# A first stage in five uneven groups of k-tiles, and a small inverse whose last transfers go through GpSimd's queue

## The chip, the cores and the metric

The kernel runs on one core of a Trainium2 chip. The metric is the device time of one execution in microseconds (us), as the median of several runs. Beside the timed runs there is one profiled execution with a trace, and a page that sums it up; all durations of single instructions come from it.

The engines are TensorE (PE, with PEld for its weight loads), VectorE (DVE), ScalarE (ACT), GpSimd (POOL) and SyncE (SP). Each works through its own queue in order. A transfer (DMA) is issued by an engine's queue: here nearly all by SP, a few by ACT. An instruction that waits holds all that stands behind it on its queue.

## What is computed

One layer of a streaming encoder on 512 prompt tokens and 64 sample tokens, of width 2048, all in float32. Cut to what matters:

```
mod = silu(c) @ w_ada + b_ada             # shift and scale (sh1, sc1), four more vectors
h = rmsnorm(x, norm1) * (1 + sc1) + sh1
proj = h @ w_in                           # columns: aq, ak, av, ar, alr, bq, bk, bv, bg, ...
o_a = GLA(aq, ak, av, gates)              # 4 heads, 64-frame blocks
o_b = GDN(bq, bk, bv, gates)              # 8 heads, each with a triangular solve (I + L)^-1
x = x + g1 * (concat(o_a, o_b) @ w_out)
x = x + g2 * conv_ffn(rmsnorm(x, norm2) * (1 + sc2) + sh2)
y = rmsnorm(x, final_norm)
```

A float32 product is made of three products of parts: each operand is split into a high part in fp32r and a low rest, and high x high, high x low and low x high are summed in PSUM.

## The kernel before, in words

Weights and activations are tiled in k-tiles of 128 rows; D = 2048 gives 16 of them. The 576 tokens are two halves of 288 columns. The function mm6 multiplies one weight tile (128x128, split in wh and wl) with one k-tile of h (split in hh and hl): six matmuls of 288 columns.

**The first stage** is the function head. It does three things at once:

- x: five blocks of tokens (four of 128, one of 64) are loaded, squared on ACT for the mean square (x_square, L765), scaled on DVE (x_scale, L769 to L772, with a power on POOL between) and turned by PE (x_turn, L780), with copies out of PSUM by ACT (L783) and DVE (L785, L788). The result is xT, x transposed.
- Modulation: the first 4096 columns of w_ada (shift and scale for norm1) are loaded in tiles called hraw, 512 KB each, from a pool of N_HRAW buffers. The generator modulation(g) does, for one group of columns, eight steps: each multiplies four k-tiles (L830), then the sums are copied out, turned, reduced, and the biases are added (L838 to L846).
- Early products: six heads of the projection (EARLY: one of bq, three of aq, two of ak) are multiplied here, in pairs of heads. They need h, made by make(k) (split_mod, L664 to L668) out of xT and of the modulation of k's own group.

Because the modulation of a group of k-tiles is enough for the products over these k-tiles, the stage goes by groups: four groups of four k-tiles. While group g is multiplied, modulation(g + 1) is stepped between the products (next(mods)). Weights of a pair are loaded by pair_load (L934) and split by pair_split (L942, L943); w_ahead(n) says how many pairs are asked for. The sums over groups are added by sum_early (L952, L957), and at the last group the results are stored (L959, L960). A narrow product (narrow_w, mm_narrow, L1050) gives the gates. load_vectors loads seven groups of small vectors by rows (v_load, L702) and turns them into columns by PE (v_turn, L710, L711).

**The mixers** follow, from about 184 to 1150 us. Weight tiles go through wtile (load L737 by SP, split on ACT and DVE, multiplied by mm6), and after each mm6 a planner is called (tick). It keeps an estimated clock, steps the jobs (generators of the heads' work) when their estimated times are due, and so writes one fixed order of instructions for every engine. Its estimate of a transfer is DMA_US + n x ISSUE_US per wait, in the function moved. The rest of w_ada's columns is summed beside it on DVE (ada_blocks; loads L976 by SP).

Each GDN head inverts a triangular 128x128 matrix. Its 16x16 diagonal blocks are inverted on POOL in inverse16: the matrix is stored to DRAM (L411), its blocks are loaded so that 32 blocks lie in 32 partitions (L418), fourteen pairs of steps run on POOL (L425, L426, shown at the helper's line L1961), a copy makes the transposed inverse (L428), then both are stored to DRAM (d1, L430) and loaded in another order into the tile cm (L435), which DVE spreads into the tiles u and t (L441, shown at L1931). PE goes on with them (shown at L1947). There are nine such inverses: eight heads and one for the samples. All of these transfers are issued by SP's queue:

```
nc.sync.dma_start(d1.rearrange("w q f -> q w f"), lane)
...
for w in range(2):
    nc.sync.dma_start(cm[:, w], d1[w].rearrange("(b n) (i j) -> (n i) b j", b=4, i=16))
```

POOL also makes the powers of every norm (rsqrt, L151) and masks; the wrapper _InTurn (L1961) keeps all of these in program order.

tc.issue_after(ins) puts what is traced inside it behind ins on the queue of the engine of ins. It is an order of issue on that one engine; it adds no wait for another.

## Time and profile before

| what | value |
|---|---|
| median of 3 runs | 2891.37 us (2891.16 to 2893.65) |
| profiled execution | 2892.92 us, span 2890.8 us |
| mean granted TensorE clock | 0.987 |
| busy share PE, PEld | 97%, 95% |
| busy share DVE, ACT, POOL | 71%, 41%, 11% |
| instructions | 52029 |
| moved by transfers | 395.53 MB, 137 GB/s on average |

The span goes from the first to the last instruction; the execution's own time is 2.1 us longer. Busy shares are averages over stages with different limits. In rows of stretches stand the stretch, its length, then for PE, PEld, DVE, ACT and POOL the busy time and the number of instructions, then the granted TensorE clock (1.00 is full), the busy share of the 16 DMA engines and GB/s. Rows of the timeline have start, duration, engine, line, operation, output <- inputs, count, and in brackets the idle time before and what ended it. In rows that group instructions stand the shapes, the count, then busy us and mean ns of one, then idle time. Rows of one tile show minimum, median and maximum in ns. Names such as "m" or "bank" are those of tiles, their numbers left out.

### The profile page before, as it was taken

The numbers are of one execution on the slowest core, as the hardware profiler recorded it, in microseconds if no ns is written. First come the engines' busy times: TensorE is split into PE (matmuls) and PEld (weight loads), VectorE is DVE, ScalarE is ACT, GpSimd is POOL, SyncE is SP. The second block draws the span as 40 slices with busy tenths as digits, with TensorE's granted clock in tenths as the row PEclk, the third lists the DMA queues.
The fourth block names the chain that finished last, engine by engine and source line by source line (L and its number), as shares of the span: only waits on it lengthen the run. The fifth ranks groups of instructions, "written<-read, shape, count | busy, mean of one in ns | idle before, by whom it ended". The sixth has DMA issues, their size and how long they took to land.

```text
span 2890.8 us, 52029 instructions
## 1 busy us (share of the span) xinstructions
PE 2811.7 (97%) x20964; PEld 2733.9 (95%) x20964; DVE 2059.6 (71%) x3305; ACT 1185.4 (41%) x2031; POOL 330.1 (11%) x513
## 2 busy tenths in 40 slices
PE   6999999999999999999999999999999999999998
PEld 3799999999899989999999999999999999999997
DVE  3468787688787783478888888888888855555555
ACT  4246544453544442454444444444444422212123
POOL 0003252323020000000111111111111000000000
PEclk8999999999999999999999999999999999999999
DMA  8966446545655555433333333333333553333221
GB/s 293 309 180 182 140 141 184 142 131 168 187 144 147 165 152 149 145 98 108 106 102 113 107 108 100 108 108 112 108 100 108 192 176 100 111 104 113 84 79 66
DMA packets 535444, 395.53 MB, mean 137 GB/s; under 512 B 59657, under 2 KB 465412, under 8 KB 535204
## 3 DMA queue, kind: packets, MB, share of 16 engines
q1 hardware_dynamic: 527860, 390.54, 44.9%
q8 instruction: 165, 2.70, 0.4%
q10 hardware_dynamic: 7344, 1.67, 0.3%
q14 instruction: 75, 0.61, 0.1%
HBM read 356.47 MB, written 35.67 MB: 136 GB/s over the span
## 4 chain that ended last, share of the span: by engine, by line
PE 87%; DVE 3%; DMA 3%; POOL 3%; issue 2%; ACT 1%; SPq 0%; ACTq 0%; POOLq 0%; DVEq 0%
PE g L641 29%; PE g L643 14%; PE bank L1584 12%; PE bank L1583 11%; PE bank L1585 11%; PE bank L1947 5%; POOL m L1961 3%; PE bank L1943 1%; DVE acc L1931 1%; PE bank L830 1%; DVE wl L1931 1%; DMA m<-gd 0%; ACT m L1907 0%; DMA raw<-in_w_in_dram 0%; PE ps_nar L1050 0%
## 5 line engine op out<-in xcount | busy, mean ns | idle before, releaser
L1584 PE MATMUL bank<-slot,wh 128*128 128x290 f32 x2464 | 739.0, 300 | 0.0
L1583 PE MATMUL bank<-slot,wh 128*128 128x290 f32 x2464 | 735.1, 298 | 0.0
L1585 PE MATMUL bank<-slot,wl 128*128 128x290 f32 x2464 | 728.8, 296 | 0.0
L641 PE MATMUL g<-slot,wh 128*128 128x288 f32 x3168 | 551.6, 295 | 0.3 <-DVE slot L1931 0.3
L641 PE MATMUL g<-hh,wh 128*128 128x288 f32 x2048 | 474.7, 313 | 5.4 <-ACT wh L1931 4.4
L1585 PEld LDWEIGHTS bank<-slot,wl 128*128 128x128 f32 x2464 | 471.8, 191 | 0.0
L1584 PEld LDWEIGHTS bank<-slot,wh 128*128 128x128 f32 x2464 | 468.8, 190 | 0.1
L641 PEld LDWEIGHTS g<-slot,wh 128*128 128x128 f32 x3168 | 464.2, 188 | 0.7 <-DVE slot L1931 0.5
L1583 PEld LDWEIGHTS bank<-slot,wh 128*128 128x128 f32 x2464 | 463.9, 188 | 0.1
L1931 ACT ACTIVATE wh<-raw 128x1024 fp32r<-128x1024 f32 x215 | 227.6, 1059 | 545.5 <-PE g L641 537.6
L641 PE MATMUL g<-hl,wh 128*128 128x288 f32 x2048 | 443.4, 298 | 0.0
L643 PE MATMUL g<-hh,wl 128*128 128x288 f32 x2048 | 443.2, 298 | 0.0
L1931 DVE SCALAR_TENSOR_TENSOR slot<-g,mod,slot 128x512 f32<-128x512 f32 (+1 forms) x448 | 201.7, 491 | 304.2 <-PE g L643 303.0
L641 PEld LDWEIGHTS g<-hh,wh 128*128 128x128 f32 x2048 | 328.4, 191 | 28.4 <-issue 14.2
L643 PE MATMUL g<-slot,wl 128*128 128x288 f32 x1584 | 342.1, 295 | 0.0
L641 PEld LDWEIGHTS g<-hl,wh 128*128 128x128 f32 x2048 | 332.9, 190 | 3.4 <-issue 2.5
L643 PEld LDWEIGHTS g<-hh,wl 128*128 128x128 f32 x2048 | 330.9, 190 | 2.4 <-issue 2.4
L1931 DVE TENSOR_TENSOR wl<-raw,wh 128x1024 fp32r<-128x1024 f32 x215 | 262.5, 1221 | 28.1 <-ACT wh L1931 25.1
L1530 ACT ACTIVATE wh<-raw 128x1024 fp32r<-128x1024 f32 x176 | 186.1, 1057 | 225.7 <-PE bank L1584 190.1
L643 PEld LDWEIGHTS g<-slot,wl 128*128 128x128 f32 x1584 | 255.5, 188 | 0.0
L1531 DVE TENSOR_TENSOR wl<-raw,wh 128x1024 fp32r<-128x1024 f32 x176 | 215.3, 1223 | 54.1 <-ACT wh L1530 54.1
L1530 ACT ACTIVATE wh<-s 128x1024 fp32r<-128x1024 f32 x132 | 140.2, 1062 | 210.5 <-DVE s L1541 109.2
(319 smaller groups left out, 3316.9 us busy)
## 6 DMA issues: line engine op xcount, KB each, us to landing
raw<-in_w_up_dram SPq DMA_DIRECT2D x176, 512.0 KB
raw<-in_w_in_dram SPq DMA_DIRECT2D x100, 512.0 KB
raw<-in_w_down_dram SPq DMA_DIRECT2D x88, 512.0 KB
aw<-in_w_ada_dram SPq DMA_DIRECT2D x71, 512.0 KB
hraw<-in_w_ada_dram SPq DMA_DIRECT2D x64, 512.0 KB
xr<-in_w_ada_dram SPq DMA_DIRECT2D x57, 512.0 KB
raw<-in_w_out_dram SPq DMA_DIRECT2D x32, 512.0 KB
slot<-actd SPq DMA_DIRECT2D x44, 288.0 KB
```

The lines of the kernel that those rows point to most:

```text
L641: T.matmul(ps[:, h if bank is None else bank, :n], wh, x[:, h, :n], start=f, stop=False)
L643: T.matmul(ps[:, h if bank is None else bank, :n], wl, ah[:, h, :n], start=False, stop=stop)
L830: T.matmul(ps[32 * k:32 * k + 32], cs[:, k0 + k], got[n][k // 2][:, k % 2], start=(k0 == 0), stop=(k0 == KD - 4))
L1530: self.nc.scalar.activation(hi, src, AF.Copy)
L1531: self.nc.vector.tensor_tensor(lo, src, hi.bitcast(F32), op=ALU.subtract)
L1583: T.matmul(ps, wh[:, j], hi, start=(c < 3 and j == 0), stop=False, skip_group_check=True)
L1584: T.matmul(ps, wh[:, j], lo, start=False, stop=False, skip_group_check=True)
L1585: T.matmul(ps, wl[:, j], hi, start=False, stop=(j == NPAIR - 1), skip_group_check=True)
L1931: return f(*a, **kw)
L1943: return self.engine.transpose(out, *a)
L1947: return self.engine.matmul(out, *a, **kw)
L1961: r = f(*a, **kw)
```

## The change

The first stage: GROUPS makes five groups of 2, 3, 4, 4 and 3 k-tiles. Group 0 then needs 256 columns each of scale and shift; its w_ada tiles hold four k-tiles of 256 columns, the others two k-tiles of the group's width. There are nine hraw buffers for eight, and ada_fill asks for w_ada as far as eight of them reach, with the weights of the next group's pairs put between (w_ahead). The first pair of weights and the narrow weights are asked for before x is squared. x_scale is cut in two (x_norm: mean and power; x_scale: four multiplications on DVE); x_square runs two blocks ahead; issue_after fixes that x's transposes come behind the last modulation step, that ACT's copies come behind a given number of squares, and that the next block's scaling on DVE comes in the middle of a block's turn. Modulation steps are spread evenly over the products (ten calls over a group). Vector group 1 is loaded later, groups 2 to 6 during the first two groups of products, into other places.

The inverse: the store of d1 and the loads of cm are issued by GpSimd's queue, the loads in four pieces instead of two. What the planner is told (moved) stays as it was.

The diff, cut to its core (what is left out does the same with the group's width and place in transposes, sums, pair_split and narrow_w, which becomes narrow_load and narrow_split):

```diff
@@ -38,13 +38,14 @@
...
-N_HRAW, HRAW_AHEAD = 8, 3
+N_HRAW = 9
...
+GROUPS = ((0, 2), (2, 3), (5, 4), (9, 4), (13, 3))
@@ -427,12 +428,14 @@
...
-        nc.sync.dma_start(d1.rearrange("w q f -> q w f"), lane)
+        nc.gpsimd.dma_start(d1.rearrange("w q f -> q w f"), lane)
...
-            nc.sync.dma_start(cm[:, w], d1[w].rearrange("(b n) (i j) -> (n i) b j", b=4, i=16))
+            for h in range(2):
+                nc.gpsimd.dma_start(cm[:, w, 2 * h:2 * h + 2],
+                                    d1[w, 16 * h:16 * h + 16].rearrange("(b n) (i j) -> (n i) b j", b=2, i=16))
@@ -763,40 +767,48 @@
...
-        def x_scale(b):
+                squared.append(last())
...
+        def x_norm(b):
...
+        def x_scale(b):
+            n, m = P if b < 4 else TS, ms[b]
...
-        def x_turn(b):
+        def x_turn(b, middle):
...
-                    T.transpose(ps[:, (k - k0) * n:(k - k0 + 1) * n], xt[b][k // 4][:n, k % 4 * P:(k % 4 + 1) * P],
-                                self.c["ident"][:n, :n])
+                    with self.tc.issue_after(summed[0]) if summed else nullcontext():
+                        T.transpose(ps[:, (k - k0) * n:(k - k0 + 1) * n], xt[b][k // 4][:n, k % 4 * P:(k % 4 + 1) * P],
+                                    self.c["ident"][:n, :n])
...
-                if b < 4:
-                    put(xT[:, k0:k0 + per, b // 2, (b % 2) * P:(b % 2 + 1) * P], ps.rearrange("p (k t) -> p k t", k=per))
-                else:
-                    for h in range(2):
-                        put(xT[:, k0:k0 + per, h, HP:HT], ps.rearrange("p (k h t) -> p k h t", k=per, h=2)[:, :, h])
+                ahead = 4 * b + (8 if k0 // per < 2 else 10)
+                with self.tc.issue_after(squared[min(len(squared), ahead) - 1]):
+                    if b < 4:
+                        put(xT[:, k0:k0 + per, b // 2, (b % 2) * P:(b % 2 + 1) * P], ps.rearrange("p (k t) -> p k t", k=per))
+                    else:
+                        for h in range(2):
+                            put(xT[:, k0:k0 + per, h, HP:HT], ps.rearrange("p (k h t) -> p k h t", k=per, h=2)[:, :, h])
+                if k0 // per == 1 and middle is not None:
+                    with self.tc.issue_after(last()):
+                        middle()
...
+        self.load_consts(self.cp, LONG)
...
-        self.load_consts(self.cp, LONG)
...
-        v_load(1)
...
-        v_turn(1)
@@ -807,19 +819,33 @@
...
-        todo = [(g, mi, k0) for g in range(4) for mi in (1, 0) for k0 in range(0, KD, 4)]
+        todo = [(g, mi, k0) for g in range(len(GROUPS)) for mi in (1, 0) for k0 in range(0, KD, 4)]
...
+        per_tile = lambda g: 4 if GROUPS[g][1] == 2 else 2
...
-                c0 = mi * D + g * 512
-                got[j] = [hraw().rearrange("p (k n) -> p k n", k=2) for _ in range(2)]
+                (m0, nm), per = GROUPS[g], per_tile(g)
+                c0, w = mi * D + m0 * P, nm * P
+                got[j] = [hraw()[:, :per * w].rearrange("p (k n) -> p k n", k=per) for _ in range(4 // per)]
...
-                    k1 = k0 + 2 * h
-                    nc.sync.dma_start(raw, i["w_ada"][0, k1 * P:(k1 + 2) * P, c0:c0 + 512].rearrange("(k p) n -> p k n", p=P))
+                    k1 = k0 + per * h
+                    nc.sync.dma_start(raw, i["w_ada"][0, k1 * P:(k1 + per) * P, c0:c0 + w].rearrange("(k p) n -> p k n", p=P))
...
+        def ada_fill():
+            while len(got) < len(todo):
+                if len(got) % 8 == 0:
+                    g = len(got) // 8
+                    w_ahead(3 if g == 1 else 3 * g - 2)
+                held = sum(len(x) for x in got.values() if x)
+                if held + 4 // per_tile(todo[len(got)][0]) > N_HRAW - 1:
+                    return
+                ada_ahead(len(got) + 1)
...
+            (m0, nm), per = GROUPS[g], per_tile(g)
+            w = nm * P
@@ -827,51 +853,60 @@
...
-                        T.matmul(ps[32 * k:32 * k + 32], cs[:, k0 + k], got[n][k // 2][:, k % 2], start=(k0 == 0), stop=(k0 == KD - 4))
+                        T.matmul(ps[32 * k:32 * k + 32, :w], cs[:, k0 + k], got[n][k // per][:, k % per], start=(k0 == 0), stop=(k0 == KD - 4))
...
+                summed[:] = [last]
...
-                ada_ahead(n + 1 + HRAW_AHEAD)
+                ada_fill()
...
-        first = modulation(0)
-        ada_ahead(1)
-        x_load(3)
-        ada_ahead(2)
-        x_load(4)
-        for g in (2, 3, 4):
-            v_load(g)
-        late = [lambda: v_turn(2), lambda: v_turn(3), lambda: v_load(5), lambda: v_turn(4), lambda: v_load(6), lambda: v_turn(5), lambda: v_turn(6)]
-        for b in range(5):
-            if b == 0:
-                x_square(0)
-            x_scale(b)
-            if b < 4:
-                x_square(b + 1)
-            x_turn(b)
-            if b > 0:
-                next(first)
-        for _ in first:
-            pass
...
-        pairs = [(g, e) for g in range(4) for e in range(0, len(EARLY), 2)]
...
+        pairs = [(g, e) for g in range(len(GROUPS)) for e in range(0, len(EARLY), 2)]
...
-                raws[j] = self.pair_load([off + h * P for _, off, h in EARLY[e:e + 2]], 4 * g)
+                raws[j] = self.pair_load([off + h * P for _, off, h in EARLY[e:e + 2]], *GROUPS[g]), GROUPS[g][1]
...
+        first, summed = modulation(0), []
+        ada_ahead(2)
+        x_load(3)
+        x_load(4)
+        ada_ahead(4)
+        v_load(1)
+        ada_ahead(7)
+        w_ahead(1)
+        nar = self.narrow_load(*GROUPS[0])
+        x_square(0)
+        x_norm(0)
+        x_scale(0)
+        x_square(1)
+        for b in range(5):
+            if b < 4:
+                x_norm(b + 1)
+            if b < 3:
+                x_square(b + 2)
+            x_turn(b, (lambda b=b: x_scale(b + 1)) if b < 4 else None)
+            if b > 0:
+                next(first)
+            if b == 3:
+                v_turn(1)
+        for _ in first:
+            pass
+        nar = self.narrow_split(pool, nar)
+        late = [lambda g=g: v_turn(g) for g in range(2, 7)]
@@ -883,26 +918,34 @@
...
-        nar = self.narrow_w(pool, 0)
-        for g in range(4):
-            mods = modulation(g + 1) if g < 3 else iter(())
-            ks = range(4 * g, 4 * g + 4)
+        for g, (m0, nm) in enumerate(GROUPS):
+            ks = range(m0, m0 + nm)
+            end = g == len(GROUPS) - 1
+            mods = iter(()) if end else modulation(g + 1)
+            units = nm * len(EARLY)
+            done = stepped = 0
...
+            def product(e, j, k):
+                nonlocal done, stepped
+                self.mm6(ps[j], w[j][0][:, k - m0], w[j][1][:, k - m0], self.h[k], k == m0, k == ks[-1])
+                done += 1
+                while stepped < 10 and stepped * (units - nm) < 10 * done:
+                    next(mods, None)
+                    stepped += 1
...
-                w = self.pair_split(raws[3 * g + e // 2])
+                w = self.pair_split(*raws[3 * g + e // 2])
...
-                        self.mm_narrow(k, nar[:, k % 4])
+                        self.mm_narrow(k, nar[:, k - m0])
...
-                            self.mm6(ps[j], w[j][0][:, k % 4], w[j][1][:, k % 4], self.h[k], k == 4 * g, k == 4 * g + 3)
+                            product(e, j, k)
...
-                        next(mods, None)
-                        if late:
-                            late.pop(0)()
-                    if g == 3:
+                    if end:
@@ -910,38 +953,39 @@
...
-                    if e == 4 and g < 3 and j == 0:
-                        nar = self.narrow_w(pool, 4 * g + 4)
+                    if e == 4 and not end and j == 0:
+                        nar = self.narrow_split(pool, self.narrow_load(*GROUPS[g + 1]))
...
-                        if e == 4 and g < 3 and j == 1 and k % 2 == 0:
-                            make(4 * g + 4 + k % 4 // 2)
-                        self.mm6(ps[j], w[j][0][:, k % 4], w[j][1][:, k % 4], self.h[k], k == 4 * g, k == 4 * g + 3)
-                        if k % 2 == 1:
-                            next(mods, None)
-                        if k == ks[1]:
-                            if late:
-                                late.pop(0)()
-                            if j == 0:
-                                w_ahead(3 * g + e // 2 + 3)
+                        if e == 4 and not end and j == 1 and k - m0 < 2:
+                            make(len(self.h))
+                        product(e, j, k)
+                        if g == 0 and e == 4:
+                            v_load(2 + 2 * j + k)
+                        if g == 1 and e == 2 and late:
+                            late.pop(0)()
+                        if k == ks[1] and j == 0:
+                            w_ahead(3 * g + e // 2 + 3)
...
+            if g == 0:
+                v_load(6)
...
-    def pair_load(self, offs, k0):
...
-        raw = self.raw()
+    def pair_load(self, offs, k0, n):
...
+        raw, w = self.raw(), n * P
...
-            self.nc.sync.dma_start(raw[:, e * 512:(e + 1) * 512].rearrange("p (k n) -> p k n", k=4), self.w_in(off)(k0, k0 + 4))
+            self.nc.sync.dma_start(raw[:, e * w:(e + 1) * w].rearrange("p (k n) -> p k n", k=n), self.w_in(off)(k0, k0 + n))
...
-    def pair_split(self, raw):
...
-        nc = self.nc
-        hi, lo = [self.wq.tile([P, 1024], F32R, tag="w" + c, bufs=3, name=self.name("w" + c)) for c in "hl"]
+    def pair_split(self, raw, n):
...
+        nc, w = self.nc, n * P
+        hi, lo = [self.wq.tile([P, 1024], F32R, tag="w" + c, bufs=3, name=self.name("w" + c))[:, :2 * w] for c in "hl"]
...
-            nc.scalar.activation(hi, raw, AF.Copy)
-            nc.vector.tensor_tensor(lo, raw, hi.bitcast(F32), op=ALU.subtract)
-        return [[x[:, e * 512:(e + 1) * 512].rearrange("p (k n) -> p k n", k=4) for x in (hi, lo)] for e in range(2)]
+            nc.scalar.activation(hi, raw[:, :2 * w], AF.Copy)
+            nc.vector.tensor_tensor(lo, raw[:, :2 * w], hi.bitcast(F32), op=ALU.subtract)
+        return [[x[:, e * w:(e + 1) * w].rearrange("p (k n) -> p k n", k=n) for x in (hi, lo)] for e in range(2)]
```

33 lines of the change are left out of this document (18 added, 15 removed).

## The prediction

> **What bounds the kernel now.** I read the page first: engine shares, then the chain that ended last.
>
> ```profile
> PE 2811.7 (97%) x20964; PEld 2733.9 (95%) x20964; DVE 2059.6 (71%) x3305; ACT 1185.4 (41%) x2031; POOL 330.1 (11%) x513
> ...
> PE 87%; DVE 3%; DMA 3%; POOL 3%; issue 2%; ACT 1%; SPq 0%; ACTq 0%; POOLq 0%; DVEq 0%
> ```
>
> TensorE is the bound, so only its idle time and its slow-clock time can be won. Busy time by stretch, up to the end of the early products (PE, PEld, DVE, ACT, POOL, then granted clock, DMA share, GB/s):
>
> ```profile
> 24.00:63.40 39.40, 25.93 (x142) 10.29 (x134) 14.62 (x37) 12.92 (x30) 1.09 (x2) 0.72 0.85 282
> 63.40:150.00 86.60, 86.58 (x609) 65.34 (x610) 35.42 (x66) 19.05 (x27) 1.09 (x3) 0.98 0.94 314
> 63.40:184.20 120.80, 119.22 (x836) 95.12 (x837) 54.46 (x95) 26.22 (x36) 1.09 (x3) 0.97 0.80 260
> ```
>
> From 63.4 us on PE is full; what runs before, shown from 24 us on, is transposes and modulation at a granted clock of 0.72, and no product. Both parts of the change aim at what is left: this start, and PE's waits in the mixers. The second place, waits from 150 to 1150 us (total, times, longest):
>
> ```profile
> PE bank L1947 <- ACT sq L1907: 11.3, 2, 10.3
> PE bank L1947 <- DVE conv_in L1931: 6.8, 2, 4.5
> ...
> PE bank L1947 <- DVE st L1907: 3.4, 1, 3.4
> ```
>
> and the same question to SP's queue:
>
> ```profile
> SPq L430 <- POOL m L1961: 109.6, 9, 20.6
> ```
>
> Nine times SP stands at the inverse's store, 12.2 us on average and 20.6 at worst, and every load behind it stands too.
>
> **Part 1, the first stage: when can the first product start?** The chain of waits, then the timeline:
>
> ```profile
> 52.93 9.36 DMA raw<-in_w_in_dram
> ...
> 63.42 2.29 PE g L641 x8
> ```
>
> ```profile
> 41.41 0.76 DVE L788 COPY xT<-g 128x256 f32<-128x256 f32 x2 [0.93 <-PE g L780]
> ...
> 52.01 1.07 PE L830 MATMUL bank<-hraw,cs 128*32 128x512 f32 x8 [1.05 <-DMA hraw<-in_w_ada_dram]
> 52.26 6.32 SPq L934 DMA_DIRECT2D raw<-in_w_in_dram  x4
> ...
> 55.03 1.15 ACT L664 ACTIVATE tmp<-xT,mod,s 128x512 f32<-128x512 f32 x2 [13.82 <-DVE mod L963]
> ...
> 56.09 1.24 ACT L667 ACTIVATE hh<-tmp 128x576 fp32r<-128x576 f32 x2
> ```
>
> The last modulation step of group 0 ends at 53.1, the operand hh is there by 56.7, yet the product waits until 63.4: its weights were asked for only at 52.26. The change asks for them before x is squared, so these 6.7 us go. It also halves what group 0 needs, from 8.4 MB of w_ada (1024 columns x 2048 rows x 4 bytes) to 4.2 MB. What has landed, in the first 41 us and in the first 160:
>
> ```profile
> DMA packets 6610, 11.47 MB, mean 280 GB/s; under 512 B 664, under 2 KB 1231, under 8 KB 6607
> ```
>
> ```profile
> DMA packets 37933, 45.52 MB, mean 285 GB/s; under 512 B 6127, under 2 KB 19235, under 8 KB 37923
> ```
>
> The first product of the new kernel needs x (16 loads of 256 KB, 4 of 128 KB: 4.7 MB), constants and two small vector groups (0.3), 4.2 of w_ada, one pair of weights (0.3): 9.5 MB, 2.0 less than had landed at 41 us. At the 395 GB/s that this row shows, that is 36 us:
>
> ```profile
> 30.00:40.00 10.00, 6.36 (x30) 3.78 (x30) 3.92 (x10) 3.85 (x10) 0.54 (x1) 0.67 1.03 395
> ```
>
> Moving the five later vector groups behind the first products takes some 10 small issues out of SP's way (I take 1 us). A last step (1 us), then 3.6 us from its end to hh (53.1 to 56.7): **40 us** for the first product, against 63.4. x must keep up, which the new order is for; ACT's part of it:
>
> ```profile
> L765 ACT ACTIVATE hs<-hs 128x512 f32<-128x512 f32 x16 | 10.0, 627 | 3.5 <-DMA hs<-in_x_prompt_dram 3.1
> ...
> L765 ACT ACTIVATION_READ_ACCUMULATOR hs<-hs 128x1 f32 x16 | 3.0, 188 | 0.0
> ...
> L783 ACT ACTIVATE xT<-g 128x512 f32<-128x512 f32 x8 | 4.8, 597 | 12.1 <-PE g L780 12.0
> ```
>
> The 20 squares at 0.63 plus 0.19 for the read and 9 copies at 0.6 are 22 us, so ACT could be through well before 36 us; x ends at 42.2 now because the engines stand in turn for one another (ACT idled 12 us ahead of these copies, waiting for the transposes, and the transposes stood in PE's queue behind modulation steps). If x slips, the first product slips by as much.
>
> From the first product on, PE's own work counts:
>
> ```profile
> 73.56 0.99 PE bank L830 x8
> ```
>
> ```profile
> L830 PE MATMUL bank<-hraw,cs 128*32 128x512 f32 x168 | 24.5, 605 | 0.0
> ```
>
> ```profile
> 183.21 0.43 PE L641 MATMUL g<-hh,wh 128*128 128x288 f32 x2
> 183.48 0.42 PE L641 MATMUL g<-hl,wh 128*128 128x288 f32 x2
> ```
>
> ```profile
> 185.00 0.53 SPq L959 DMA_DIRECT2D early_aq<-acc  x1
> ```
>
> The last early product's store is issued at 185.0, behind its eviction; the product itself ends about 184.2, where I cut the stretch above. Two products start per 0.265 us: 576 + 64 narrow ones are 85 us in both kernels. Of the modulation 168 records, 21 steps of 8, lie behind the first product now, about 1.1 us each with their issue: 23. Together 108 of 120.8; 12.8 go to transposes, to the slow clock at the start and to the three group borders. Afterwards all 32 steps of groups 1 to 4 lie behind the first product, of 384, 512, 512 and 384 columns: 8 x (0.75 + 1 + 1 + 0.75) x 0.99 + 32 x 0.11 = 31; the 12.8 become 15.5 with a fourth border. Sum 131.5: the stage ends at 171.5 instead of 184.2, **12.7 us earlier**. The start is 23 us earlier and pays only 13, because 8 us of steps and a border that now fill an idle PE then lie between products. The six further evictions fall on DVE in a stretch where it is busy 45% (54.46 of 120.8), cover enough; the split copies shrink with the group. SP issues 16 loads more (72 of w_ada for 64, 30 of weights for 24, 10 narrow for 8); at the 0.42 us of an issue (the cm row below) that is 7 us of SP in 130, hidden as long as SP runs ahead of the transfers; without that cover it would be 7 us at the end of the stage. The issue-order rules hold no engine for another: each orders one engine's own queue. SP meets its first wait for a w_ada buffer when all nine are in use, by when group 0 is asked for whole. The moved vector loads and their transposes only change place: groups 2 to 6 are needed by nothing in this stage.
>
> **Part 2, the small inverse.** The longest stall, at 718 to 729 us (SP, then POOL, then all engines by stretch):
>
> ```profile
> 701.65 0.38 SPq L976 DMA_DIRECT2D aw<-in_w_ada_dram  x1
> 719.09 0.32 SPq L430 DMA_DIRECT2D d<-m  x1
> ...
> 722.26 0.86 SPq L1230 DMA_DIRECT2D out_dram<-sq  x2
> ```
>
> ```profile
> 697.92 20.49 POOL L1961 TENSOR_TENSOR m<-m 32x14 f32<-32x14 f32 x28
> ```
>
> ```profile
> 725.00:730.00 5.00, 1.34 (x7) 1.34 (x7) 0.00 (x0) 3.85 (x7) 0.00 (x0) 0.50 1.00 322
> 730.00:735.00 5.00, 5.00 (x32) 5.00 (x32) 3.67 (x9) 3.97 (x8) 0.00 (x0) 0.77 0.04 9
> ```
>
> POOL's 28 steps last to 718 (and DVE, ACT and PE ran dry by then); behind the store waits the conv state's store (L1230), whose tile a later ACT copy wants, and PE queues on that copy. On POOL's own queue the store needs no wait, and SP goes on. I count the 10.3 us whole and 1.8 for the clock (1.34 us at 0.50, 5 at 0.77): 12. The waits of 4.5, 3.4 and 2.3 at 556, 453 and 296 follow the same blocks, while DVE works off a burst of late loads; DVE is also busy by itself, so I count half, 5. Next late there is DVE.
>
> What it adds: five issues on POOL for three on SP, and POOL stands until the store has landed. No DMA from POOL is in this trace. The nearest rows, on that tile and of SP's loads:
>
> ```profile
> L435 SPq DMA_DIRECT2D cm<-d x18: 364/417/518, 269.5 to 839.0; - x18
> ```
>
> ```profile
> L1961 POOL TENSOR_TENSOR m<-m x252: 202/502/4403, 248.2 to 836.0; 32x14 f32<-32x14 f32 x18, 32x26 f32<-32x26 f32 x18, 32x36 f32<-32x36 f32 x18, 32x44 f32<-32x44 f32 x18
> ...
> L1961 POOL COPY m<-m x9: 591/989/1076, 266.8 to 836.3; 32x256 f32<-32x256 f32 x9
> ```
>
> An issue costs between 0.36 us (SP's) and 4.4 (POOL's slowest step); I take 1.0, POOL's copy of the same data. Then cm comes 4 us later and POOL is held 6.6 us (1.6 of landing, 5 issues). Queued behind it on POOL are the next heads' powers and masks, and on them ACT, DVE and PE. How late may cm be?
>
> ```profile
> 303.60 0.33 SPq L430 DMA_DIRECT2D d<-m  x1
> 305.26 0.93 SPq L435 DMA_DIRECT2D cm<-d  x2
> 308.52 0.69 DVE L1931 TENSOR_TENSOR m<-cm,consts 128x512 f32<-128x512 f32 x1 [0.38 <-DMA cm<-d]
> ...
> 329.83 0.28 PE L1947 MATMUL bank<-m,m 128*128 128x64 f32 x1
> ```
>
> Even where DVE waits for cm itself, PE asks 21 us later. I charge 3 us over all nine for late powers. Net **14 us**.
>
> The Trainium skill, SBUF — State Buffer, section "SBUF: two separate sides", warns of this part: DVE in a two-port mode keeps GpSimd from writing its DMA's descriptors, 620 ns becoming about 3,100. By that the issues would be 15.5 us an inverse instead of 5. Nothing in this trace shows it.
>
> **Sum.** The profiled execution took 2892.9 us (span 2890.8), the median of the runs is 1.6 lower. 2892.9 - 12.7 - 14 = 2866.2; for the median **2864.5 us**.
>
> **Rivals.**
> - The loads bind the first stage. Behind 40 us there remain 34 MB; at 282 GB/s, the rate of 24 to 63 us, they end at 161, and 20 us of last group (4 us of modulation, 3 x 40 products) end at 181: 3 gained. For it: shares of 0.94 from 63 to 150 us, and runs of 1 and 1.5 KB instead of 2. Against: the 395 GB/s of 30 to 40 us, with 1.03 of the engines' share. 2874 us.
> - The first stage gains, the queue gains nothing: DVE, not SP, held the mixers, or late powers eat the 17. 2878.5 us.
> - Both better: product at 36, every wait after a block gone (22), POOL free of cost: 2850 us.
> - **Slower**: POOL's issues are slow beside a busy DVE. At 4.4 us, five last 22 us, powers of the other heads queue behind, and PE's fixed order waits at them. It decides from 30 / 9 = 3.3 us of PE wait per inverse; at 8 us each, 72 - 30 = 42 more: 2933 us. For it: POOL's steps reach 4.4 us. Against: 21 us of slack and a median of 0.5. The skill's rule above would be one way to it.
>
> **How the numbers follow.** Forecast 0.55; loads bind 0.14; queue gains nothing 0.12; both better 0.10; slower 0.09. The range takes 2846 (the better case and 4 us) to 2888 (the forecast with every issue bound high). A measurement here can tell 0.2%, 5.8 us, from no change. Faster 0.87, same 0.05, slower 0.08.
>
> **What would show it.** Right: the first g<-hh,wh product at 36 to 44 us, early stores of the last group near 172, no SP wait on POOL's m, no idle stretch of 10 us near 715, cm loads on POOL near 1 us. Wrong: PE waits on hraw or on xT after 40 us, PE waits named kt, rq or m<-cm in the mixers, or a mixer stage longer from its first product to its end than before.

## The result and the profile after

The changed kernel takes **2903.16 us** (median of 5 runs, 2901.80 to 2912.74) against 2892.59 us (2891.16 to 2894.26) for the kernel before, run in turn with it. The ratio is 1.0047, with a 95% interval of 1.0033 to 1.0060: slower by half a per cent, where 2864.5 us and a gain were forecast.

The page of the changed kernel gives the engine shares, then GpSimd's new DMA queue (packets, MB, share), then the chain that ended last.

```profile
PE 2818.2 (97%) x21028; PEld 2737.3 (94%) x21028; DVE 2064.6 (71%) x3322; ACT 1185.6 (41%) x2035; POOL 355.0 (12%) x559
...
q0 software_dynamic: 1440, 1.18, 0.2%
...
PE 77%; DVE 3%; POOL 2%; issue 2%; DMA 2%; ACT 1%; SPq 0%; ACTq 0%; POOLq 0%; DVEq 0%
```

The shares hardly moved, though the span grew by 9.3 us (2900.1 against 2890.8). So both kernels have to be laid side by side in time. The table takes the same PE instruction in both traces and gives its start after the change, less its start before:

| PE instruction (start before) | after less before |
|---|---|
| first early product g<-hh,wh (63.42) | -24.2 us |
| bank<-consts,qkv, behind the first stage (243.10) | -5.7 |
| bank<-m,m at the wait on conv_in (556.08) | +16.9 |
| bank<-sq,m, where the longest stall stood (728.66) | +9.3 |
| g<-hh,wh at the wait on wh (1066.49) | +11.9 |
| end of the span (2890.8) | +9.3 |

Four things can be read: the start is gained, three quarters of it are lost again inside the first stage, the mixers then lose 22.6 us up to 573, and about 10 of these come back at the old stall.

**The first stage.** PE's timeline at the first product, and at the first border between groups (in brackets the idle time before the instruction, and what ended it):

```profile
38.90 0.45 PE L1098 MATMUL ps_nar<-hh,nar 128*66 128x288 f32 x2 [2.58 <-ACT hh L670]
39.18 0.43 PE L644 MATMUL g<-hh,wh 128*128 128x288 f32 x2
```

```profile
64.36 0.85 PE L644 MATMUL g<-hh,wh 128*128 128x288 f32 x2 [2.06 <-ACT hh L670]
```

The columns of the next answer are those of the stretches before: PE, PEld, DVE, ACT, POOL, clock, DMA share, GB/s.

```profile
39.00:63.40 24.40, 22.60 (x156) 13.38 (x155) 4.84 (x12) 6.22 (x11) 0.32 (x1) 0.93 1.02 347
63.40:100.00 36.60, 31.91 (x202) 21.24 (x203) 15.64 (x32) 6.37 (x11) 0.32 (x1) 0.91 0.95 310
100.00:150.00 50.00, 49.41 (x360) 36.05 (x359) 24.62 (x46) 9.77 (x14) 0.72 (x2) 1.00 0.85 273
```

```profile
179.40 0.53 SPq L1003 DMA_DIRECT2D early_aq<-acc  x1
```

From 39 to 100 us the transfers run at 0.95 to 1.02 of their share, PE is idle for 6.5 us of 61, and its clock is 0.91 to 0.93. Before the change PE was full from 63.4 us on, at 0.98. The last early store goes out at 179.40 instead of 185.00: 5.6 us gained.

**The mixers.** PE's waits from 150 to 1150 us, then two lines of the same question to DVE's queue (200 to 900 us):

```profile
PE bank L1995 <- DVE m L1979: 12.5, 2, 6.8
PE bank L1995 <- DVE conv_in L1979: 5.3, 2, 4.1
PE bank L1995 <- DVE sq L1955: 4.8, 6, 2.1
PE g L644 <- ACT wh L1979: 4.1, 1, 4.1
PE bank L1995 <- POOL m L2009: 3.6, 1, 3.6
```

```profile
DVE kt L1955 <- POOL kt L2009: 29.6, 9, 9.6
...
DVE m L1979 <- DMA cm<-d: 10.3, 4, 4.4
```

The wait on ACT's sq (11.3 us in 2 before) is down to 0.9. New are PE's wait on POOL's m and DVE's on cm. Longer are PE's wait on DVE's m (0.8 us before) and DVE's on kt (8.3 us in 9 before), the power that POOL makes for the next head. SP's wait at the inverse's store (109.6 us in 9) is gone too.

These waits are not the whole loss. The same PE work in both traces, from the instruction at 243.10 us to those at 556.08 and 1066.49, first before, then after the change:

```profile
243.10:556.08 312.98, 300.22 (x2331) 293.25 (x2331) 247.64 (x441) 154.14 (x395) 113.54 (x176) 0.99 0.55 158
243.10:1066.49 823.39, 792.85 (x6093) 768.90 (x6093) 654.26 (x1219) 395.79 (x922) 199.85 (x332) 0.99 0.53 154
```

```profile
237.40:572.95 335.55, 309.76 (x2330) 301.71 (x2331) 246.50 (x441) 153.55 (x395) 123.44 (x201) 0.95 0.51 148
237.40:1078.43 841.03, 802.39 (x6093) 775.54 (x6093) 654.22 (x1219) 394.99 (x922) 225.30 (x377) 0.98 0.52 151
```

Of the 22.6 us lost in the first stretch, 13.0 are idle time of PE (25.8 for 12.8). The other 9.5 are the same instructions taking longer, 309.76 us for 300.22, at a granted clock of 0.95 for 0.99. Over the whole stretch 17.6 us are lost: 8.1 idle and again 9.5 busy.

GpSimd's timeline of one inverse shows where the new waits come from:

```profile
670.05 0.63 POOL L431 DMA_DIRECT2D d<-m  x1 [0.32 <-POOL m L2009]
673.53 0.74 POOL L437 DMA_DIRECT2D cm<-d  x1 [2.85 <-DMA d<-m]
677.24 0.72 POOL L437 DMA_DIRECT2D cm<-d  x1 [2.96 <-issue]
679.84 0.73 POOL L437 DMA_DIRECT2D cm<-d  x1 [1.88 <-issue]
682.23 0.72 POOL L437 DMA_DIRECT2D cm<-d  x1 [1.66 <-issue]
682.97 1.05 POOL L2009 TENSOR_TENSOR kt<-kt,mhalf 128x4 f32<-128x4 f32 x1
```

```profile
L437 POOL DMA_DIRECT2D cm<-d x36: 720/729/757, 266.6 to 854.7; - x36
...
  issue: 63.7, 28
...
DMA to landing us min/median/max: 2.0/2.1/4.3
```

One issue takes 0.73 us (all 36 lie between 0.72 and 0.76). But between two loads the queue stands, mostly 1.6 to 3.9 us and 59.0 us in 27 gaps (the 63.7 us in 28 hold one wait of 4.7 before a first load). So their starts lie 2.3 to 4.6 us apart; a load lands in 2.0 to 4.3 us, 2.1 at the median. From the store to the last load pass 9.6 to 16.9 us, in this inverse 12.2. The power kt, queued behind it, starts right after the last load. At the first inverse, where they pass 16.9 us, DVE and then PE wait for cm itself:

```profile
281.48 0.69 DVE L1979 TENSOR_TENSOR m<-cm,consts 128x512 f32<-128x512 f32 x1 [4.18 <-DMA cm<-d]
```

### The profile page after: what moved, and what is told of

The parts are those of the page before. It is cut to its first block, busy times and chain, and to the rows that moved or that the text cites. A ratio compares the mean times of both kernels' runs of the same rounds, so it can differ in the third digit from the quotient of the medians.

```text
span 2900.1 us, 52292 instructions
## 1 busy us (share of the span) xinstructions
PE 2818.2 (97%) x21028; PEld 2737.3 (94%) x21028; DVE 2064.6 (71%) x3322; ACT 1185.6 (41%) x2035; POOL 355.0 (12%) x559
## 4 chain that ended last, share of the span: by engine, by line
PE 77%; DVE 3%; POOL 2%; issue 2%; DMA 2%; ACT 1%; SPq 0%; ACTq 0%; POOLq 0%; DVEq 0%
PE g L644 25%; PE g L646 12%; PE bank L1632 12%; PE bank L1631 11%; PE bank L1633 11%; PE bank L1995 4%; POOL m L2009 1%; PE bank L1991 1%; DVE acc L1979 1%; DVE wl L1979 1%; DMA d<-m 0%; POOL cm L437 0%; PE bank L1841 0%; ACT wh L1979 0%; DMA raw<-in_w_down_dram 0%
```

## The experiments

The theories. **A**: GpSimd's queue stands between the loads of cm, cm and whatever is queued behind it come late, and that costs the mixers some 20 us. **A1**: it stands because the memory set aside for the descriptors of its transfers holds one load's only (dynamic_dma_scratch_size is 512 in both kernels), so that the former must land first. **A2**: it stands because DVE keeps GpSimd from writing. **B**: the new order of the first stage shifts the mixers' work. For the lost part of the first stage, **D**: the borders of small groups; **E**: the loads bind; **F**: the order of PE's instructions.

Each ratio is to the kernel before on the same chip, with its 95% interval. The last two columns are the median of the kernel and that of the kernel before beside it.

| run | ratio (95%) | us | before |
|---|---|---|---|
| first stage alone | 0.9976 (0.9966 to 0.9985) | 2886.43 | 2892.88 |
| second part alone | 1.0082 (1.0068 to 1.0096) | 2916.37 | 2892.88 |
| both, 1920 bytes, 3 tiles s0 | 0.9979 (0.9970 to 0.9988) | 2887.01 | 2892.88 |
| both, only the store on GpSimd | 0.9966 (0.9953 to 0.9978) | 2883.31 | 2892.88 |
| both, 896 bytes | 0.9963 (0.9950 to 0.9975) | 2883.97 | 2894.41 |
| first stage alone, steps sooner | 0.9970 (0.9961 to 0.9979) | 2885.94 | 2894.41 |
| first stage alone, half of w_ada | 0.9916 (0.9901 to 0.9932) | 2870.92 | 2894.41 |
| first stage alone, four groups of 4 | 0.9968 (0.9955 to 0.9980) | 2885.25 | 2894.41 |
| first stage alone, all bytes, half used | 0.9967 (0.9954 to 0.9980) | 2883.26 | 2893.32 |
| second part alone, 896 bytes | 0.9966 (0.9954 to 0.9979) | 2883.36 | 2893.32 |
| both, 1152 bytes, 3 tiles ts | 0.9961 (0.9948 to 0.9974) | 2880.83 | 2893.32 |
| both, 1920 bytes, 2 tiles sl | 0.9960 (0.9948 to 0.9972) | 2881.86 | 2893.32 |

### The first stage alone

```diff
-        nc.gpsimd.dma_start(d1.rearrange("w q f -> q w f"), lane)
+        nc.sync.dma_start(d1.rearrange("w q f -> q w f"), lane)
...
-            for h in range(2):
-                nc.gpsimd.dma_start(cm[:, w, 2 * h:2 * h + 2],
-                                    d1[w, 16 * h:16 * h + 16].rearrange("(b n) (i j) -> (n i) b j", b=2, i=16))
+            nc.sync.dma_start(cm[:, w], d1[w].rearrange("(b n) (i j) -> (n i) b j", b=4, i=16))
```

> The changed kernel with the inverse's store and its two loads back on SP's queue: the new first stage alone. Theory A (the GpSimd queue stands between the loads of cm, and what is queued behind them on GpSimd comes late): the stage keeps its 5.6 us and the mixers are those of before, so 2892.6 - 5.7 = 2887 us (2884 to 2890), and the stall of 10 us near 720 us is back. Rival B (it is the new order of the first stage that shifts the mixers' work and costs them 15 us): still about 2902 us, with waits of PE on m<-cm or conv_in between 280 and 570 us.

It is 6.4 us faster than before, as A has it; B falls. SP stands at the store again, and the old stall is back:

```profile
SPq L431 <- POOL m L2007: 111.3, 9, 20.6
```

```profile
727.29 1.22 PE L1993 MATMUL bank<-sq,m 128*128 128x128 f32 x4 [10.97 <-ACT sq L1953]
```

### The second part alone

```diff
-        nc.sync.dma_start(d1.rearrange("w q f -> q w f"), lane)
+        nc.gpsimd.dma_start(d1.rearrange("w q f -> q w f"), lane)
...
-            nc.sync.dma_start(cm[:, w], d1[w].rearrange("(b n) (i j) -> (n i) b j", b=4, i=16))
+            for h in range(2):
+                nc.gpsimd.dma_start(cm[:, w, 2 * h:2 * h + 2],
+                                    d1[w, 16 * h:16 * h + 16].rearrange("(b n) (i j) -> (n i) b j", b=2, i=16))
```

> The kernel before with the store and four loads of the inverse on GpSimd's queue: the second part alone. Theory A: the mixers lose what they lost in the changed kernel, from 5.7 us early to 9.3 us late, 15 us: 2907.5 us (2902 to 2912); loads of cm 2.4 to 4.6 us apart. Rival B: no loss without the new first stage, 2893 us or less.

It is 23.5 us slower than before, more than the 15 that A expected, so the two parts do not simply add up. DVE's waits and those of POOL's queue:

```profile
DVE kt L1909 <- POOL kt L1963: 36.8, 9, 11.7
...
DVE m L1933 <- DMA cm<-d: 8.1, 2, 4.3
```

```profile
POOL cm L436 <- issue: 61.9, 28, 4.1
```

### More room: 1920 bytes

```diff
-    nc = bacc.Bacc("TRN2", target_bir_lowering=False, num_devices=1, dynamic_dma_scratch_size=512)
+    nc = bacc.Bacc("TRN2", target_bir_lowering=False, num_devices=1, dynamic_dma_scratch_size=1920)
...
-        st = k.sp.tile([P, 256], F32, tag="s0", bufs=4, name=k.name("s0"))[:, :self.w]
+        st = k.sp.tile([P, 256], F32, tag="s0", bufs=3, name=k.name("s0"))[:, :self.w]
```

> The changed kernel with dynamic_dma_scratch_size 1920 instead of 512; the state tiles s0 have 3 buffers instead of 4, which makes the room in SBUF for it. Theory A1 (each load waits because the 512 bytes hold the descriptors of one load only, so that the former has to land first): the four loads of cm follow one another at about 0.8 us, the last is issued within 7 us of the store instead of 10 to 17, and the time falls by 10 to 20 us to 2883 to 2893 us or below. Theory A2 (a busy DVE keeps GpSimd from writing its descriptors, as the Trainium skill, SBUF — State Buffer, section SBUF: two separate sides, has it): the spacing stays 2.4 to 4.6 us, and the time stays at 2903 us.

A1 holds: the four loads go out in one row, and the queue's standing falls from 63.7 us in 28 to 3.9 in 1, which is before a first load. DVE no longer waits for cm.

```profile
296.73 0.59 POOL L431 DMA_DIRECT2D d<-m  x1 [0.29 <-POOL m L2009]
300.49 2.88 POOL L437 DMA_DIRECT2D cm<-d  x4 [3.16 <-DMA d<-m]
```

The ratio falls from 1.0047 to 0.9979, though this kernel loses 8 us between 880 and 950 us that the others above do not. A2 falls: DVE's work is the same, the median issue takes 0.72 us as before, and the gaps are gone.

### More room without another edit: 896 bytes

```diff
-    nc = bacc.Bacc("TRN2", target_bir_lowering=False, num_devices=1, dynamic_dma_scratch_size=512)
+    nc = bacc.Bacc("TRN2", target_bir_lowering=False, num_devices=1, dynamic_dma_scratch_size=896)
```

> The changed kernel with dynamic_dma_scratch_size 896 instead of 512 and nothing else. Theory A1 (the 512 bytes hold one load's descriptors): with 896 two or three loads go out together and the wait between them comes once per inverse instead of three times, so that the last load is issued 6 to 9 us after the store; the time is between 2903 and 2887 us, nearer the lower end, about 2885 to 2890. If the loss of 8 us between 880 and 950 us in the run with 1920 bytes came from its three state buffers, it is not here and the time is 2878 to 2884 us. If a load fills more than half of 896 bytes, spacing and time stay as in the changed kernel, 2903 us.

Three loads go together, the fourth waits:

```profile
300.20 2.16 POOL L437 DMA_DIRECT2D cm<-d  x3 [3.18 <-DVE acc L1979]
303.84 0.72 POOL L437 DMA_DIRECT2D cm<-d  x1 [1.47 <-issue]
```

One number in the kernel turns 0.5% slower into 0.4% faster. The loss between 880 and 950 us is not there; the last pair of runs below comes back to it.

### Only the store on GpSimd

```diff
-            for h in range(2):
-                nc.gpsimd.dma_start(cm[:, w, 2 * h:2 * h + 2],
-                                    d1[w, 16 * h:16 * h + 16].rearrange("(b n) (i j) -> (n i) b j", b=2, i=16))
+            nc.sync.dma_start(cm[:, w], d1[w].rearrange("(b n) (i j) -> (n i) b j", b=4, i=16))
```

> The changed kernel with only the inverse's last store on GpSimd; cm is read by two loads on SP, as before the change. Theory A (A1 and A2 alike): SP no longer stands at the store, and no load of cm stands on GpSimd: the 15 us are back and the stall of 10 us near 720 us stays away, 2875 to 2888 us, SP waiting 2 to 4 us per inverse for the store to land. Rival B: about 2902 us. Rival C (what SP gains by not standing at the store is lost elsewhere in any case): 2887 us, as the first part alone.

The time is inside A's range, but by another way than it said, and its interval overlaps that of the first stage alone: rival C, no gain from the store, fits as well. SP stands at the loads now nearly as long as it stood at the store (109.6 us in 9), and the stall of 10 us stays:

```profile
SPq L436 <- DMA d<-m: 90.3, 9, 18.5
```

```profile
728.14 1.22 PE L1993 MATMUL bank<-sq,m 128*128 128x128 f32 x4 [10.64 <-ACT sq L1953]
```

A load that needs the store's data waits for all that the store waits for. To free SP, the loads must leave its queue too.

### The first stage: steps sooner

```diff
-                while stepped < 10 and stepped * (units - nm) < 10 * done:
+                while stepped < 10 and stepped * (units - nm - 6) < 10 * done:
```

> The first stage alone (inverse on SP's queue), with the ten pieces of the next group's modulation through six products sooner within each group. Theory D (the way from the last modulation step to the next group's hh, some 5 us, does not fit behind the last two to four products of a small group, and PE idles there and runs slowly after): the waits of PE on hh at 64 and 100 us go and the stage ends 3 to 5 us earlier, 2882 us against 2886.4 for the first stage alone. Theory E (loads bind: the steps then wait for hraw instead): no gain, 2886 us or more, with PE waits on hraw.

The wait at the second border (1.25 us at 99.56 in the changed kernel) goes, the one at the first stays (2.06 us at 66.16), so the edit tests D at one border only. The last store goes out at 179.09, and the time is that of the first stage alone. D falls as the main cause.

### The first stage: half of w_ada, and all of it with half used

```diff
-                got[j] = [hraw()[:, :per * w].rearrange("p (k n) -> p k n", k=per) for _ in range(4 // per)]
+                got[j] = [hraw()[:, :per * w].rearrange("p (k n) -> p k n", k=per) for _ in range(4 // per if g == 0 else 1)]
...
-                        T.matmul(ps[32 * k:32 * k + 32, :w], cs[:, k0 + k], got[n][k // per][:, k % per], start=(k0 == 0), stop=(k0 == KD - 4))
+                        T.matmul(ps[32 * k:32 * k + 32, :w], cs[:, k0 + k], got[n][k // per if g == 0 else 0][:, k % per], start=(k0 == 0), stop=(k0 == KD - 4))
```

> The first stage alone (inverse on SP's queue); from the second group on only the first half of each modulation step's rows of w_ada is loaded and used twice, so the scale and shift of these groups are not the reference's; the work of PE is unchanged and about 6.3 MB of loads are gone. Theory E (loads bind the stage between 40 and 100 us): the stage ends 5 to 8 us earlier, 2879 to 2882 us. Theory D (borders of small groups and the slow clock behind them): the waits on hh at 64 and 100 us stay, and the time is 2885 to 2887 us.

The second kernel has only the second of these edits.

> As the run that loaded only the first half of each later modulation step's rows of w_ada and used it twice (2870.9 us), but with both halves loaded again, the second unused: the modulation of the later groups is again not the reference's, PE's work is that of both earlier kernels, the bytes are those of the first stage alone. Theory E (the bytes set the stage): back to the first stage alone, 2885 to 2888 us, with DMA at 97% of its share from 39 to 100 us. Theory F (not the bytes, but the order of PE's instructions, which moved with the smaller loads): it stays near 2871 to 2875 us.

From 39 to 100 us, the first stage alone, then half of w_ada, then all bytes with half used:

```profile
39.00:100.00 61.00, 54.38 (x355) 34.61 (x355) 20.22 (x43) 12.38 (x20) 0.64 (x2) 0.92 0.98 328
```

```profile
39.00:100.00 61.00, 61.00 (x434) 41.35 (x433) 27.50 (x55) 15.13 (x24) 1.36 (x4) 0.98 0.81 248
```

```profile
39.00:100.00 61.00, 56.82 (x378) 36.85 (x377) 23.62 (x50) 14.76 (x23) 0.64 (x2) 0.94 1.00 348
```

With half the bytes PE never idles, its clock is 0.98, and the last early store goes out at 165.37 instead of 179.93, 14.6 us earlier, more than E expected. With all the bytes back and PE's work unchanged it goes out at 176.17: 10.8 of the 14.6 us go again with the bytes. The time, 2883.26 us, lies a little below E's range and far from F's. The other 3.8 go with which half of each step is used, and with PE's order, which is not quite the same in the three kernels; these two were not told apart.

### The first stage: four groups of 4

```diff
-GROUPS = ((0, 2), (2, 3), (5, 4), (9, 4), (13, 3))
+GROUPS = ((0, 4), (4, 4), (8, 4), (12, 4))
...
-                        if g == 0 and e == 4:
+                        if g == 0 and e == 4 and k < 2:
```

> The first stage alone (inverse on SP's queue) with four groups of 4 k-tiles instead of 2, 3, 4, 4 and 3, and with the new order of loads and of x's work. The first product then needs 4.2 MB more of w_ada and comes at about 52 us; 8 modulation steps and one border fewer lie behind it. Theory D: by 85 us of products, 23 of steps and 12.8 of the rest the stage ends at 173 us, 5 us before that of the five groups: 2881 us. Theory E: the stage ends with the loads, at 178 us as with five groups or later, 2886 us or more.

The first product waits for the loads until 53.16, 14 us later than with five groups, and the stage still ends 2 us earlier (last store 177.99); the time is the same within the interval:

```profile
50.76 1.93 PE L854 MATMUL bank<-hraw,cs 128*32 128x512 f32 x8 [2.44 <-DMA hraw<-in_w_ada_dram]
...
53.16 1.16 PE L642 MATMUL g<-hh,wh 128*128 128x288 f32 x4
```

An earlier first product is not what sets the end. E holds.

### The second part alone with 896 bytes

The edit of the second part alone, and

```diff
-    nc = bacc.Bacc("TRN2", target_bir_lowering=False, num_devices=1, dynamic_dma_scratch_size=512)
+    nc = bacc.Bacc("TRN2", target_bir_lowering=False, num_devices=1, dynamic_dma_scratch_size=896)
```

> The kernel before with the inverse's store and four loads on GpSimd's queue and dynamic_dma_scratch_size 896, so without the new first stage: what the second part is worth where the loads need not wait for one another. From the chip: the stall of 10 us near 728 us gone, some 5 us lost again at 290 to 320 and near 552 us, so 3 to 5 us faster than before, 2889 to 2891 us against 2893 to 2894. By the prediction's own sum (17 gained, 3 lost) it would be 2879 to 2880 us.

It is 10.0 us faster than before, more than expected from the runs. The trace shows the stall gone, but at 1066 us the kernel is only 0.5 us ahead; 6.2 of the profiled 6.7 us (spans 2890.8 and 2884.1) come behind that, where nothing was changed (see the last section). So the time is sure, its place is not, and it is not shown that all of it comes from the inverse.

### The best version, and 1920 bytes taken from elsewhere

```diff
-    nc = bacc.Bacc("TRN2", target_bir_lowering=False, num_devices=1, dynamic_dma_scratch_size=512)
+    nc = bacc.Bacc("TRN2", target_bir_lowering=False, num_devices=1, dynamic_dma_scratch_size=1152)
...
-        t = self.sp.tile([P, TS], F32, tag="ts", bufs=4, name=self.name("ts"))
+        t = self.sp.tile([P, TS], F32, tag="ts", bufs=3, name=self.name("ts"))
```

> The changed kernel with dynamic_dma_scratch_size 1152, the room taken from the small tiles ts (3 buffers instead of 4). Theory A1: four loads of cm fit, the fourth follows the third without a wait, the last is issued 5 to 7 us after the store; GpSimd is free 2 us sooner per inverse than with 896 bytes: 2879 to 2884 us. If the fourth load's wait cost nothing, as with 896 bytes, 2884 us.

All four loads go together, and the power follows them at once; the whole change now gains 0.39%, 0.26 to 0.52%:

```profile
301.56 2.88 POOL L437 DMA_DIRECT2D cm<-d  x4 [2.50 <-DVE acc L1979]
304.47 1.06 POOL L2009 TENSOR_TENSOR kt<-kt,mhalf 128x4 f32<-128x4 f32 x1
```

The second kernel has 1920 bytes, all four tiles s0, and

```diff
-                sn = self.sp.tile([P, 256], F32, tag="sl", bufs=3, name=self.name("sl"))
+                sn = self.sp.tile([P, 256], F32, tag="sl", bufs=2, name=self.name("sl"))
```

> As the run with 1920 bytes, but the room is taken from the tiles sl (2 buffers instead of 3) and the state tiles s0 keep 4. If the 8 us lost between 880 and 950 us in that run came from s0, they are not lost here: 2877 to 2881 us. If they came from the faster loads themselves, 2885 to 2888 us as there.

At 887 us it is 11.4 us ahead of the kernel before, at 925 only 6.8: some of the loss between 880 and 950 stays, so s0 was not all of it. The traces show most of it. The same 15 us with 1152 bytes, with 1920 and 3 tiles s0, and with 1920 and 2 tiles sl:

```profile
880.00:895.00 15.00, 14.05 (x109) 12.89 (x108) 8.71 (x18) 12.46 (x24) 0.00 (x0) 1.00 0.34 97
```

```profile
880.00:895.00 15.00, 13.43 (x67) 11.10 (x66) 7.24 (x18) 10.12 (x20) 0.00 (x0) 0.66 0.32 93
```

```profile
880.00:895.00 15.00, 14.75 (x80) 13.36 (x81) 5.73 (x15) 11.18 (x23) 0.00 (x0) 0.66 0.33 96
```

With 1920 bytes PE is busy there at a granted clock of 0.66. By an estimate (busy time x 0.34) that costs 4.6 us with 3 tiles s0, over half of the loss of 8, and 5.0 with 2 tiles sl, all of the loss of 4.6. What lowers the clock is open: with 2 tiles sl it falls behind a wait of 0.94 us on ACT's sq, and with 1152 bytes PE waits 0.94 us at the same instruction and stays at 1.00.

The two runs beat both kernels, and cannot be told from each other or from 896 bytes.

## Why the prediction was wrong, point by point

- **First product at 40 us**: 39.18. Right.
- **Stage 12.7 us earlier**: 5.6 in the trace, 6.4 us in the runs of the first stage alone. The step that failed is the sum from the first product on, which counted PE's work and took transfers to keep up ("the 12.8 become 15.5"). PE's work was not too small: with half the bytes the stage from first product to last store takes 126.5 us (38.83 to 165.37), less than the 131.5 forecast, and in the changed kernel 140.2. The missing time is PE's idling and slow clock while the loads bind, from 39 to 100 us. The rival "the loads bind the first stage" had the mechanism: 34 MB behind 40 us, and an end at 181. That its end came out so near is partly luck: the last loads of the stage were asked for at 149.4 us, where it had them end at 161, and what followed took longer than its 20 us. I had set against it one row of 395 GB/s; the stage's own stretches show 347, 310 and 273.
- **The stall at 718 to 729 us, 12 us**: right. In the changed kernel the product stands 9.3 us late where just before, at 716, it was 19.8 late: 10.5 come back. With 896 bytes the two numbers are -2.8 and +7.7. In every run with the loads on SP the stall stays, 10.6 to 11.5 us.
- **Half of the waits at 556, 453 and 296, 5 us**: not there. With 1152 bytes, where SP no longer stands at the store, PE still waits 2.23, 2.86 and 2.27 us for DVE at these places, and 4.94 more at 551. So freeing SP does not end them, as the rival "the queue gains nothing" had it for this part; how much of DVE's lateness there is now its wait for kt was not separated.
- **An issue at 1.0 us, so cm 4 us late and POOL held 6.6**: this step turned the sign. The issue takes 0.73 us, inside its bounds. But the sum took a load to cost its issue alone. Between two loads stood the landing of the former, which no bound covered, and POOL was held 10 to 17 us. With room for more loads and nothing else changed (896 bytes) the kernel is faster than before, so this step alone decides the sign.
- **21 us of slack for cm**: not enough at the first inverse, where DVE waits for cm until 281.48 and PE then waits 5.7 us for m. PE's other wait for m, 6.8 us at 565, is not for cm itself: its last load was issued at 547.27, and DVE, late by a wait of 8.5 us on ACT's wh, comes to m only at 563.96.
- **3 us for late powers**: too small, as far as the traces go. DVE waits 29.6 us for kt in the changed kernel and 8.2 in the first stage alone; how much of that reaches PE was not measured.
- **The clock behind new waits**: the sum put it at nothing; it counts a slow clock only at the stall of 718 us. The mixers lose 9.5 us by it up to 573 us, beside 13.0 of idling.
- **The rival "slower"** had the right form (POOL holds, powers queue behind, PE waits) with the wrong cause, a busy DVE. Its turning point was 3.3 us per inverse, against a gain of 30 us: from 243 to 692 us (by the times before the change) the kernel goes from 5.7 ahead to 19.9 behind, and by 875 another 4.7 are lost (7.6 to 12.3 behind); that is 30.3 us in nine inverses, 3.4 each. The loss met the turning point almost exactly; the kernel is clearly slower because only some 16 of the 30 us were gained (5.7 by 243 us and 10.5 at the old stall).
- **Two figures beside the sum**: the rival "both better" adds up to 2852.6 us (2892.9 - 16.7 - 22 - 1.6), not 2850, and the range's end of 2888 does not follow from the bound of 4.4 us that it names. Neither changes the outcome.

The Trainium skill, SBUF — State Buffer, section "SBUF: two separate sides", has an operation of DVE in a two-port mode stretch such a DMA from 620 to about 3100 ns. The 15.5 us an inverse estimated from that lie inside the 10 to 17 measured by chance, for the runs do not show that cause: the 36 loads of the changed kernel took 0.72 to 0.76 us each beside a DVE that is busy 71% of the time, and the gaps between them went with the room, not with DVE.

The Trainium skill, DMA: Bandwidth & Descriptors, section "SWDGE vs HWDGE vs iDMA", says that GpSimd appends its descriptors to rings in a part of SBUF set aside for them. No trace shows the rings, but the runs agree: with more of this memory more loads went out together, and with room for one each waited for the former to land.

How the parts add up is not settled. Alone they gain 6.4 (first stage) and 10.0 us (second, with 896 bytes), together 10.4. Some 6 of the 10.0 may belong to a stretch that neither part touches (last section); without them the parts would add up, but one trace cannot settle that. In the profiled execution of the first stage alone the 5.4 us won at 243 are 1.0 at 1066, handed back at the waits at 291, 451, 554 and 727, as what ends these does not come sooner. That was read from traces, not tried. Nor was it tried how much of what the mixers still lose beside enough room comes from kt standing behind the inverse on POOL (20.2 us of DVE's waits with 1152 bytes).

## What to carry to other kernels

Before a transfer is moved to GpSimd's queue, ask how many of them the memory for its descriptors holds: with room for one, each waits for the former to land, and an engine that also computes is held with it. Moving a wait off a queue needs every instruction that hangs on it to move, the dependent load as much as the store. A stage is priced by its own rate of transfers before its engine's work is summed: an earlier start pays nothing that the loads behind it can't follow. And a new wait of PE is priced with the slow clock that was seen behind such waits, here 9.5 us beside 13.0.

## What the runs showed of the hardware

- One load of cm (256 runs of 64 bytes) takes between 257 and 288 of the bytes of dynamic_dma_scratch_size: 512 let one go at a time, 896 three, 1152 four (512 / 2 and 1152 / 4 are the ends). This is worked out from which loads went together.
- The stretch from 1306 us to the final norm has the same work in all kernels. In thirteen of the fourteen traces it lasts 1517.8 to 1520.8 us, in that of the second part alone with 896 bytes 1514.6. Kernel before, then that one:

```profile
L1507 PE MATMUL bank<-dg,consts x4: 689/689/852, 1306.0 to 1307.6; 116*128 116x290 f32 x4
```

```profile
L1798 DVE TENSOR_TENSOR y<-bank,fn x24: 669/681/692, 2826.8 to 2879.2; 128x512 f32<-128x512 f32 x16, 32x512 f32<-32x512 f32 x8
```

```profile
L1509 PE MATMUL bank<-dg,consts x4: 689/689/851, 1305.6 to 1307.3; 116*128 116x290 f32 x4
```

```profile
L1800 DVE TENSOR_TENSOR y<-bank,fn x24: 668/680/692, 2820.2 to 2872.6; 128x512 f32<-128x512 f32 x16, 32x512 f32<-32x512 f32 x8
```

From 1306.0 to 2826.8 are 1520.8 us, from 1305.6 to 2820.2 are 1514.6. The 6 us do not fall at one place. With PE full and its clock at 1.00 in both, PE starts a few instructions more in each 100 us, here 746 for 743:

```profile
1410.00:1510.00 100.00, 100.00 (x743) 100.00 (x742) 82.68 (x101) 44.23 (x54) 10.62 (x14) 1.00 0.36 103
```

```profile
1410.00:1510.00 100.00, 100.00 (x746) 100.00 (x746) 83.26 (x103) 44.76 (x54) 11.39 (x14) 1.00 0.36 102
```

What makes this is open, and whether it belongs to the kernel or to the one execution that was profiled; a place in a single trace is known no better than that over such a length.
